# Remainders of prefetched weight units: subtraction on VectorE replaced by a negated copy on ScalarE and an accumulating transfer

## The chip, the core and the metric

The kernel runs on one core of a Trainium2 chip. The metric is the device time of the whole kernel in microseconds (us). Engines are named as in the profile: PE is TensorE, DVE is VectorE, ACT is ScalarE, POOL is GpSimd, SP is SyncE. In this kernel SP computes nothing: it issues transfers, in order.

## What is computed

A decoder trunk of two layers on 512 tokens of width 1024, in float32. Cut to what matters:

```
for l in range(2):
    h = x * (1 + scale1) + shift1
    u, q, k, v = split(h @ w_in[l])                 # 512 columns each
    ssm = s5_mixer(u)                               # state space scan, GELU, GLU with glu_w (512 x 512)
    att = diff_attention(rotary(q), rotary(k), v)   # 4 heads, two softmax maps each, causal
    mix = concat(ssm, att) @ w_out[l]
    x = layer_norm(alpha * x + (1 + gate1) * mix)
    h = x * (1 + scale2) + shift2
    x = layer_norm(alpha * x + (1 + gate2) * (silu(h @ w_gate) * (h @ w_up)) @ w_down)
```

The shifts, scales and gates are columns of `silu(c) @ mod_w[l] + mod_b[l]`.

## The kernel before, in words

Each matrix product is done as three matmuls in a rounded float32 format. Every operand X is split into a rounded part `hi` and a remainder `lo = X - hi`, and `mm3` (line 115) adds hi·hi, hi·lo and lo·hi in PSUM.

The weights come as 184 units of 128 x 1024 floats (512 KB), 92 for each layer. `wunit` (line 263) makes one: SP issues the load of `wraw` (two buffers), ACT rounds it into `whi` (five buffers; the helper `cp` on line 113), and DVE subtracts, `wlo = wraw - whi` (five buffers; the helper `tt`, line 104). A table `plo` gives the subtraction of four units of layer 1 to POOL. A buffer of `wraw` is free for the next load when the subtraction has read it.

`prefetch` calls `wunit` ahead of use, for 14 units of each layer: eight for the q and k columns (two for each head; the first has the weight rows of the lower four of eight k tiles, the second those of the upper four), two for the GLU, four for the output projection. `units(n)` hands the oldest ones out. All other units, those of u, v and of the feed-forward part, call `wunit` directly.

The mixer of a layer weaves three streams: the projections (PE), the S5 scan (`s5_gen`: small matmuls `kps`, `utp`, `qps`, `vps`, `yps` with chains of DVE and POOL work between them), and attention (`att_gen`). `tick()` is called between pieces of projection and starts whatever the table `PLAN` has due: a step of `s5`, of `att`, of the modulation columns (`mod`, each a 512 KB load `mraw` and a DVE reduction), or one `pf`, a prefetch. The framework then orders the instructions of each engine by its own schedule, so the order on an engine differs from that in which the code calls them.

SP's queue carries the unit loads `wraw` (line 265), the modulation loads `mraw` (294), small transfers of the S5 scan (`M<-kd` 544, `kd<-ksb` 475, `csl<-sC` 649) and others. A transfer that must wait for a buffer or for data holds all behind it on SP. POOL issues some transfers too (`sQ`, `sG`, `xs`, `gd`).

Of the kernel before, what the change touches and what calls it, by code (L numbers as in the profile page):

```python
# [14 lines left out]
ALU = mybir.AluOpType  # L15
# [7 lines left out]
OPT = {'MQ': 'sync', 'MODQ': 'sync', 'q_bld': 1, 'q_s5': 0, 'q_att': 0, 'q_pf': 0, 'CSQ': 'scalar', 'plo': [[1, 0, 1, 0, 0, 0, 0, 0, 0, 0, 0, 0, 0, 0, 0, 0, 0, 0], [0, 0, 0, 0, 0, 0, 1, 1, 1, 0, 0, 0, 0, 1, 0, 0, 0, 0]]}  # L23
# [39 lines left out]
def trunk_kernel(tc, xT, x, c, pos, modw, modb, wst, s5a, s5bc, s5d, glub, lamv, subw, lng, lnr, out):  # L63
    nc = tc.nc
    from contextlib import ExitStack

    with ExitStack() as es:
# [35 lines left out]
        def tt(out, a, b, op, eng=None):  # L103
            (eng or nc.vector).tensor_tensor(out, a, b, op=op)  # L104
# [7 lines left out]
        def cp(out, in_, scale=1.0):  # L112
            nc.scalar.activation(out, in_, AF.Copy, scale=scale)  # L113
# [9 lines left out]
        def f(ap):  # L123
            return ap.bitcast(F32)
# [135 lines left out]
                nc.gpsimd.dma_start(kd[l][:, :, 128:240].rearrange("q p x -> p q x"), zb)  # L260


        def wunit(idx, eng=None):
            raw = wp.tile([P, 1024], F32, tag="wraw", name="wraw", bufs=2)
            nc.sync.dma_start(raw, wst[idx])
            hi = wp.tile([P, 1024], F32R, tag="whi", name="whi", bufs=5)
            cp(hi, raw)
            lo = wp.tile([P, 1024], F32R, tag="wlo", name="wlo", bufs=5)
            tt(lo, raw, f(hi), ALU.subtract, eng=eng)
            return hi, lo  # L270

        ahead = []

        def prefetch(*idx):
            ahead.extend(wunit(i, nc.gpsimd if i % W0 < 22 and OPT["plo"][i // W0][i % W0 - 4] else None) for i in idx)

        def units(n):
            r = ahead[:n]
# [603 lines left out]
        W0 = 92  # L882
# [52 lines left out]
        for l in range(L):  # L935
# [7 lines left out]
            if l == 0:  # L943
# [35 lines left out]
                with queued(marks(), (POOL,)), strict():  # L979
                    first_x(0)  # L980
                    uw[0] = wunit(wb)
                    first_h(0)
                    first_l(0)
                    first_x(1)
                    for k in range(NK):
                        kp = k // 2
                        for t in range(NT):
                            mm3(ups[t], kt(hT, k, tok(t)), rows(uw[kp], k % 2), k == 0, k == 7)
                        if k + 1 < NK:
                            first_h(k + 1)  # L990
                        if k % 2 == 0 and k + 2 < NK:
                            uw[kp + 1] = wunit(wb + kp + 1)
                        if k + 2 < NK:
                            first_x(k + 2)
                        if k + 1 < NK:
                            first_l(k + 1)
                        for c_ in START[k]:
                            if c_ == "v":
                                vw.append(wunit(wb + 4 + len(vw)))
                            elif c_ == "V":  # L1000
                                first_v()
                            elif c_ == "c":
                                s5_rot(0, rots.pop(0), pms[0])
                            elif c_ == "p":
                                next(par, None)
                            elif c_ == "r":
                                next(rope, None)
                            elif c_ == "b":
                                next(bld)
                            else:  # L1010
                                mods_bg(cols, 2, "A2")
# [36 lines left out]
            def tick():  # L1048
                while plan and plan[0][0] < now[0] + 1:
                    kind = plan.pop(0)[1]  # L1050
                    if kind == "att":
                        with queued(marks()) if OPT["q_att"] else nullcontext():
                            next(attg, None)
                    elif kind == "s5":
                        with queued(marks(), (POOL,)) if OPT["q_s5"] else nullcontext():
                            next(s5g, None)
                    elif kind == "pf":
                        with queued(marks()) if OPT["q_pf"] else nullcontext():
                            prefetch(wb + pfs.pop(0))
                    elif kind == "cs":  # L1060
                        with queued(marks() if OPT["q_bld"] else m0, (POOL,)):
                            if rots:
                                s5_rot(0, rots.pop(0), pms[0])
                    elif kind == "bld":
                        with queued(marks() if OPT["q_bld"] else m0, (POOL,)):
                            next(bld, None)
                    else:
                        mods_bg(cols, 1, now[1])
                now[0] += 1
# [292 lines left out]
```

## Time and profile before

| what | value |
|---|---|
| median of 3 runs | 1278.39 us (1275.9 to 1282.51) |
| profiled execution, its time | 1279.54 us |
| its span | 1277.8 us |
| mean granted clock of PE over the span | 0.976 of full speed |
| PE busy | 1190.9 us, 93% of the span |
| DVE busy | 841.6 us, 66% |
| ACT busy | 478.9 us, 37% |
| POOL busy | 206.4 us, 16% |

The span is the time from the first to the last recorded instruction; 1.74 us of the profiled execution's time lie outside it. The busy shares are means over stages that have different limits. The mixer of layer 0 runs until about 260 us, its feed-forward part follows; the mixer of layer 1 lies between about 690 and 865 us.

### The profile page before, as it was taken

To read this page: it belongs to the slowest core of one execution; us is meant where nothing else is said; L and a number is where in the kernel's file an instruction comes from. 1 tells how busy PE (TensorE), PEld (TensorE's weight loads), DVE (VectorE), ACT (ScalarE), POOL (GpSimd) and SP (SyncE) were. 2 spreads that over 40 slices of the span, in tenths; PEclk is the share of its full clock that TensorE was granted. 3 is DMA by queue.
4 is the path that set the end of the run, shared out by engine and by line. 5 is a ranking of instruction groups with operands and counts; after the bars stand their busy time and mean duration, and the time that the engine had idled before them with its cause. 6 is when DMAs were issued, how large, how long until landed. Compare 5 with 4: busy or idle time off the path is not lost.

```text
span 1277.8 us, 17430 instructions
## 1 busy us (share of the span) xinstructions
PE 1190.9 (93%) x6608; PEld 992.1 (78%) x6608; DVE 841.6 (66%) x1537; ACT 478.9 (37%) x846; POOL 206.4 (16%) x286
## 2 busy tenths in 40 slices
PE   4768888999999999989899999999999999999997
PEld 3557777688888888867687798878888888888885
DVE  6679999866687576698647557785666222235556
ACT  3413446527322222243346245661733222234330
POOL 8943320001002121132001131100000000000001
PEclk8887999999999999999899999999999999999999
DMA  9654236534665666744333554423463333333241
GB/s 357 226 153 143 65 82 226 158 107 152 195 221 186 226 200 193 252 141 146 117 99 101 186 168 107 131 83 99 151 196 103 98 96 100 99 99 115 66 133 66
DMA packets 66868, 186.57 MB, mean 146 GB/s; under 512 B 7936, under 2 KB 21536, under 8 KB 66784
## 3 DMA queue, kind: packets, MB, share of 16 engines
q1 hardware_dynamic: 62352, 174.88, 43.4%
q0 software_dynamic: 2848, 8.70, 2.1%
q10 hardware_dynamic: 1584, 1.88, 0.5%
q8 instruction: 52, 0.85, 0.3%
q14 instruction: 32, 0.26, 0.1%
HBM read 171.85 MB, written 11.49 MB: 143 GB/s over the span
## 4 chain that ended last, share of the span: by engine, by line
PE 68%; DVE 18%; DMA 4%; POOL 3%; issue 3%; ACT 3%; SPq 0%; DVEq 0%; POOLq 0%; ACTq 0%
PE gps L116 37%; PE dps L116 14%; PE ops L116 4%; PE vps L116 3%; DVE mraw L110 3%; PE ups L116 2%; PE qkps L116 2%; DVE wlo L104 2%; DVE stmp L104 1%; POOL s5tmp L104 1%; DMA mraw<-in_modw 1%; DMA wraw<-in_wst 1%; DVE Gt L104 1%; PE yps L116 1%; PE glups L116 1%
## 5 line engine op out<-in xcount | busy, mean ns | idle before, releaser
L104 DVE TENSOR_TENSOR wlo<-wraw,whi 128x1024 fp32r<-128x1024 f32 x180 | 225.3, 1254 | 266.3 <-ACT whi L113 264.4
L113 ACT ACTIVATE whi<-wraw 128x1024 fp32r<-128x1024 f32 x184 | 194.2, 1058 | 376.6 <-PE gps L116 273.0
L116 PE MATMUL gps<-hT2h,whi 128*128 128x512 f32 (+1 forms) x768 | 286.4, 373 | 0.2
L116 PE MATMUL gps<-hT2l,whi 128*128 128x512 f32 (+1 forms) x768 | 285.7, 372 | 0.0
L116 PE MATMUL gps<-hT2h,wlo 128*128 128x512 f32 (+1 forms) x768 | 285.3, 372 | 0.0
L116 PE MATMUL dps<-whi,ah 128*128 128x512 f32 x704 | 223.7, 397 | 8.2 <-DVE rtmp L104 4.5
L116 PEld LDWEIGHTS gps<-hT2h,whi 128*128 128x128 f32 x768 | 144.6, 188 | 25.8 <-DVE rtmp L104 0.6
L116 PEld LDWEIGHTS dps<-whi,ah 128*128 128x128 f32 x704 | 133.9, 190 | 39.5 <-DVE rtmp L104 6.0
L116 PEld LDWEIGHTS gps<-hT2h,wlo 128*128 128x128 f32 x768 | 144.7, 188 | 25.1
L116 PEld LDWEIGHTS gps<-hT2l,whi 128*128 128x128 f32 x768 | 144.7, 188 | 24.9
L116 PE MATMUL dps<-wlo,ah 128*128 128x512 f32 x352 | 138.5, 393 | 0.0
L110 DVE SCALAR_TENSOR_TENSOR mraw<-mraw,scb 128x1024 f32<-128x1024 f32 x96 | 122.0, 1299 | 1.8 <-DMA mraw<-in_modw 1.6
L113 ACT ACTIVATE ah<-aT 128x512 fp32r<-128x512 f32 x88 | 53.8, 627 | 115.5 <-PE dps L116 93.2
L104 DVE TENSOR_TENSOR ah<-aT,ah 128x512 fp32r<-128x512 f32 x88 | 61.1, 706 | 40.0 <-ACT ah L113 39.6
L116 PEld LDWEIGHTS dps<-wlo,ah 128*128 128x128 f32 x352 | 67.2, 191 | 13.6
L116 PE MATMUL qkps<-whi,hTh 128*128 128x256 f32 x128 | 39.7, 312 | 7.3 <-ACT whi L113 6.5
L116 PE MATMUL ops<-whi,am 128*128 128x512 f32 x128 | 43.4, 398 | 0.0
L116 PE MATMUL qkps<-wlo,hTh 128*128 128x256 f32 x128 | 40.0, 313 | 0.5 <-DVE wlo L104 0.5
L104 POOL TENSOR_TENSOR rs<-rs,mhalf 128x1 f32<-128x1 f32 x16 | 10.8, 676 | 176.8 <-DVE rs L101 176.8
L116 PE MATMUL qkps<-whi,hTl 128*128 128x256 f32 x128 | 39.1, 306 | 0.0
L751 ACT ACTIVATE e<-sps,nm 128x128 f32<-128x128 f32 (+3 forms) x64 | 33.1, 525 | 14.9 <-DVE nm L749 12.8
L116 PE MATMUL qkps<-whi,hTnh 128*128 128x256 f32 x128 | 37.4, 292 | 0.0
(290 smaller groups left out, 1939.4 us busy)
## 6 DMA issues: line engine op xcount, KB each, us to landing
wraw<-in_wst SPq DMA_DIRECT2D x184, 512.0 KB, 3.7
mraw<-in_modw SPq DMA_DIRECT2D x96, 512.0 KB, 4.8
M<-kd SPq DMA_DIRECT2D x64, 64.0 KB, 3.6
gb<-in_lnr SPq DMA_DIRECT2D x8, 512.0 KB, 4.1
xT<-in_xT SPq DMA_DIRECT2D x8, 256.0 KB, 7.1
u<-us SPq DMA_DIRECT2D x32, 64.0 KB, 2.5
csl<-sC SPq DMA_DIRECT2D x8, 256.0 KB, 2.8
x<-in_x SPq DMA_DIRECT2D x4, 512.0 KB, 4.1
```

Of the source, the lines that this page charges most:

```text
L104: (eng or nc.vector).tensor_tensor(out, a, b, op=op)
L110: nc.vector.scalar_tensor_tensor(out, a, s, b, op0=ALU.mult, op1=ALU.mult, accum_out=acc_out)
L113: nc.scalar.activation(out, in_, AF.Copy, scale=scale)
L116: nc.tensor.matmul(ps, a, b, start=start, stop=stop)
L751: nc.scalar.activation(e[:, m, :n], ps[:, m, :n], AF.Exp, bias=nm[:, m : m + 1], accum_out=ss[:, i, m : m + 1])
```

## The change

The 28 prefetched units get their remainder another way. ACT writes `wlo = -whi` (a copy with scale -1 of the rounded part), and POOL issues a transfer that adds `wraw` onto it in place, from SBUF to SBUF. The value is the same. The other 156 units keep the subtraction on DVE; the branch for POOL's four goes with `prefetch`'s call.

```diff
-        def wunit(idx, eng=None):
+        def wunit(idx, eng=None, dma=False):
             raw = wp.tile([P, 1024], F32, tag="wraw", name="wraw", bufs=2)
             nc.sync.dma_start(raw, wst[idx])
             hi = wp.tile([P, 1024], F32R, tag="whi", name="whi", bufs=5)
             cp(hi, raw)
             lo = wp.tile([P, 1024], F32R, tag="wlo", name="wlo", bufs=5)
-            tt(lo, raw, f(hi), ALU.subtract, eng=eng)
+            if dma:
+
+                cp(lo, f(hi), scale=-1.0)
+                nc.gpsimd.dma_start(f(lo), raw, accum_op=ALU.add)
+            else:
+                tt(lo, raw, f(hi), ALU.subtract, eng=eng)
             return hi, lo
 
         ahead = []
 
         def prefetch(*idx):
-            ahead.extend(wunit(i, nc.gpsimd if i % W0 < 22 and OPT["plo"][i // W0][i % W0 - 4] else None) for i in idx)
+            ahead.extend(wunit(i, dma=True) for i in idx)
```

The lines of the kernel after are those of before plus 5 behind this place.

The scheduler moves instructions. SP, in the mixer of layer 0, where the loads for the last head (head 3) and for the GLU stand. Before, the `wraw` x2 of the second row are both units of head 3, and the last row is the GLU's two:

```order
L475 DMA kd_125<-ksb 128x128
L265 DMA wraw<-in_wst 128x1024 x2
L544 DMA M<-kd_125 16x8x128
L649 DMA csl<-sC 128x512
L544 DMA M<-kd_125 16x8x128 x5
L294 DMA mraw<-in_modw 128x1024
L544 DMA M<-kd_125 16x8x128 x2
L294 DMA mraw<-in_modw 128x1024
L265 DMA wraw<-in_wst 128x1024 x2
```

After, `wraw` x2 is the second unit of head 2 and the first of head 3; the next single `wraw` is head 3's second, and the last row is the first of the GLU's:

```order
L265 DMA wraw<-in_wst 128x1024 x2
L480 DMA kd_125<-ksb 128x128
L549 DMA M<-kd_125 16x8x128 x3
L654 DMA csl<-sC 128x512
L549 DMA M<-kd_125 16x8x128 x4
L299 DMA mraw<-in_modw 128x1024
L549 DMA M<-kd_125 16x8x128
L265 DMA wraw<-in_wst 128x1024
L299 DMA mraw<-in_modw 128x1024
L265 DMA wraw<-in_wst 128x1024
```

Head 3's second load has moved behind all eight `M` transfers, `csl` and one `mraw`.

On POOL, at the start of layer 1's mixer, the transfers for head 0's two units stand right behind the attention's `lve`, and those of the next units where the subtractions given to POOL stood.

PE, first matmuls of head 0 in layer 1, where the k tiles 4 and 5 (second unit) follow 2 and 3 (first unit). Before (`hTnh_4885` holds k tiles 2 and 3, `hTnh_4886` 4 and 5):

```order
L116 MATMUL qkps<-wlo,hTnh_4885 128x256
L116 MATMUL qkps<-whi,hTnl_4889 128x256
L116 MATMUL qkps<-whi,hTnh_4886 128x256
L116 MATMUL qkps<-wlo,hTnh_4886 128x256
L116 MATMUL qkps<-whi,hTnl_4890 128x256
```

After (`hTnh_4898` holds k tiles 0 and 1, `hTnh_4899` 2 and 3, `hTnh_4900` 4 and 5):

```order
L116 MATMUL qkps<-wlo,hTnh_4899 128x256
L116 MATMUL qkps<-whi,hTnl_4903 128x256
L116 MATMUL qkps<-whi,hTnh_4900 128x256
L116 MATMUL qkps<-wlo,hTnh_4898 128x256
L116 MATMUL qkps<-whi,hTnl_4902 128x256
```

Before, the second unit's `wlo` is read 12 matmuls after head 0's first; now PE first takes the 12 matmuls of the first unit for a second token tile, so it is read 24 after.

## Rows read from the trace of the kernel before

**Rows 1.** The page: span, and busy time of each engine.

```profile
span 1277.8 us, 17430 instructions
PE 1190.9 (93%) x6608; PEld 992.1 (78%) x6608; DVE 841.6 (66%) x1537; ACT 478.9 (37%) x846; POOL 206.4 (16%) x286
```

**Rows 2.** Busy by stretch (from:to us): PE, PEld, DVE, ACT, POOL, clock, DMA share, GB/s.

```profile
100.00:260.00 160.00, 139.56 (x1154) 118.21 (x1153) 147.96 (x320) 78.00 (x191) 34.05 (x32) 0.95 0.45 135
740.00:860.00 120.00, 114.30 (x976) 100.44 (x975) 88.23 (x204) 67.58 (x170) 21.11 (x25) 1.00 0.43 122
```

**Rows 3.** The same view, `wlo` alone: PE, PEld, DVE, POOL, clock, DMA share, GB/s.

```profile
100.00:260.00 160.00, 48.23 (x149) 29.62 (x149) 15.82 (x13) 0.00 (x0) 0.95 0.45 135
740.00:860.00 120.00, 44.03 (x146) 27.49 (x145) 10.91 (x9) 9.75 (x4) 1.00 0.43 122
```

**Rows 4.** Groups by form: count, busy us, mean ns, idle before and its releasers.

```profile
L104 DVE TENSOR_TENSOR wlo<-wraw,whi 128x1024 fp32r<-128x1024 f32 x180 | 225.3, 1254 | 266.3 <-ACT whi L113 264.4 <-DMA M<-kd 1.5
...
L113 ACT ACTIVATE whi<-wraw 128x1024 fp32r<-128x1024 f32 x184 | 194.2, 1058 | 376.6 <-PE gps L116 273.0 <-DMA wraw<-in_wst 77.5 <-PE dps L116 10.1
...
L104 POOL TENSOR_TENSOR wlo<-wraw,whi 128x1024 fp32r<-128x1024 f32 x4 | 9.8, 2438 | 21.6 <-ACT whi L113 21.6
```

**Rows 5.** The chain of waits, layer 0's mixer: start us, us, what.

```profile
96.73 1.24 DVE wlo L104
...
180.84 1.13 DVE wlo L104
...
198.82 1.14 DVE wlo L104
```

**Rows 6.** The chain of waits, layer 1's mixer.

```profile
738.00 11.53 PE qkps L116 x96
...
777.10 1.23 DVE wlo L104
...
824.41 1.13 DVE wlo L104
```

**Rows 7.** The timeline of ACT in three places: start us, us, operation, idle before.

```profile
95.64 1.06 ACT L113 ACTIVATE whi<-wraw 128x1024 fp32r<-128x1024 f32 x1 [1.34 <-issue]
...
188.33 0.60 ACT L113 ACTIVATE qkt<-qkps 128x512 f32<-128x512 f32 x1 [1.10 <-PE qkps L116]
...
736.57 1.05 ACT L113 ACTIVATE whi<-wraw 128x1024 fp32r<-128x1024 f32 x1
```

**Rows 8.** Transfers by issue: queue, count, KB each, median us to landing.

```profile
wraw<-in_wst SPq DMA_DIRECT2D x184, 512.0 KB, 3.7
...
sQ<-Q POOLq DMA_DIRECT2D x4, 512.0 KB, 5.6
...
gd<-mods POOLq DMA_DIRECT2D x4, 4.0 KB, 10.3
```

**Rows 9.** The timeline of PE, 96 to 140 us; in brackets the idle time ahead.

```profile
98.01 0.58 PE L116 MATMUL qkps<-wlo,hTh 128*128 128x256 f32 x1 [0.47 <-DVE wlo L104]
...
112.42 0.59 PE L470 MATMUL kps<-Gt,s5bc 128*32 128x112 f32 x16 [2.16 <-DVE stmp L104]
...
116.47 1.98 PE L615 MATMUL yps<-M,UU 128*64 128x128 f32 x16 [1.30 <-ACT ksb L113]
...
136.86 0.59 PE L470 MATMUL kps<-Gt,s5bc 128*32 128x112 f32 x16 [3.87 <-DVE Gt L104]
```

**Rows 10.** SP's timeline around head 3's loads.

```profile
183.73 0.35 SPq L294 DMA_DIRECT2D mraw<-in_modw  x1
184.13 0.91 SPq L544 DMA_DIRECT2D M<-kd  x2
```

**Rows 11.** The timeline of POOL at layer 1's start.

```profile
732.20 0.72 POOL L104 TENSOR_TENSOR lve<-ebase,lvs 128x2 f32<-128x2 f32 x1 [13.17 <-DVE lvs L709]
```

**Rows 12.** PE's waits, 55 to 300 us: total us, times, longest.

```profile
PE kps L470 <- DVE Gt L104: 10.8, 3, 4.2
```

**Rows 13.** SP's waits, 90 to 260 us.

```profile
SPq L265 <- DVE wlo L104: 18.4, 7, 4.1
```

## The prediction, before the changed kernel was run

> **What bounds the kernel now.** I read the page's busy line first. PE works 93% of the span, DVE 66%, ACT 37% [rows 1], so over the whole kernel PE sets the time, and a subtraction taken off DVE is worth something only where DVE ends last. The change touches the two mixers alone, so I cut the trace there [rows 2]. In 100 to 260 us (mixer of layer 0) DVE is busy 147.96 of 160 us and PE 139.56: here DVE bounds, and PE's 20.4 us of idle time are waits for it. In 740 to 860 us (mixer of layer 1) PE is busy 114.30 of 120 and DVE 88.23: here PE bounds, and DVE has room. The feed-forward parts keep their units and their order. The same stretches for `wlo` alone [rows 3] give what DVE would lose: 15.82 us in 13 subtractions in layer 0, 10.91 us in 9 in layer 1, where POOL loses 9.75 us in 4.
>
> **What is removed.** Of 180 subtractions on DVE at 1.25 us and 4 on POOL at 2.44 us [rows 4], 24 and 4 go. The ceiling for layer 0 is the 15.8 us of DVE work, if its stream were a single one that decides throughout. With the order kept, only a subtraction that the chain of waits goes through shortens it. In layer 0 there are three of them, 1.24 + 1.13 + 1.14 = 3.5 us [rows 5]; in layer 1 two, 1.23 + 1.13 = 2.4 us [rows 6]. The other 23 lie beside other work. That makes -5.9 us. The longer DVE gain I leave to a rival, since 13 x 1.22 us taken from a stream move its end only if DVE finds its next operands ready.
>
> **What is added on ACT.** 28 copies of 128x1024, priced as the rounding copy, 1.06 us each [rows 4]: 29.7 us, half of it in each mixer. ACT is busy 78.00 of 160 and 67.58 of 120 us [rows 2], so its idle time hides them except in the path of one unit, which becomes longer: rounding, negated copy, transfer, matmul, where it was rounding, subtraction, matmul.
>
> **What a transfer takes.** No row of before has an accumulating transfer or one from SBUF to SBUF. Nearest are transfers of the same 512 KB: unit loads from SP land after 3.7 us, `sQ` from POOL after 5.6 us [rows 8]. The slowest that POOL issues is `gd`, 10.3 us [rows 8]. I take 5.6 (same size, same queue) and keep 3.7 and 10.3 as bounds, as nothing excludes either. A remainder is then ready 1.06 + 5.6 = 6.7 us after its rounding in place of 1.25 us: 5.4 us later. POOL, busy 34.05 of 160 and 21.11 of 120 us [rows 2], has time to issue 14 transfers in each; what it loses, four subtractions, is more in layer 1 than what it gets. Where units are prefetched long ahead, the 5.4 us are hidden. Three places are not like that.
>
> *Layer 0, head 0, second unit.* Its rounding ends at 95.64 + 1.06 = 96.70 us [rows 7], PE wants the remainder at 98.01 - 0.47 = 97.54 and gets it at 98.0 [rows 9]. After: 96.70 + 1.06 + 5.6 = 103.4, that is 5.4 us later than now (3.5 to 10.1 by the bounds). Right behind, PE stands idle for DVE three times, 2.16 + 1.30 + 3.87 = 7.3 us by 137 us [rows 9]. DVE doesn't wait for head 0 there, but for its own scan work, so a late PE finds these operands ready. Price 0; if the cover is gone, 5.4; at the slow bound 10.1 - 7.3 = 2.8.
>
> *Layer 0, head 3, second unit.* SP now loads it behind an `mraw` and the `M` transfers. Those were issued at 183.73 and 184.13 us [rows 10], so the load goes out at about 184.6, lands 3.7 later (188.3), is rounded and negated by 190.4 and added by 196.0. Head 2's last copy on ACT starts at 188.33 [rows 7], PE then has 12 matmuls of the first unit at 0.12 us (11.53 us for 96, rows 6) and wants the remainder at 189.8: 6.2 us of waiting (4.3 to 10.9 by the bounds). But with DVE lighter, what SP waits for at the `M` transfers comes earlier, too. I take half, +3.1, with ends 0 and 10.9.
>
> *Layer 1, head 0.* POOL can't issue before `lve` ends, 732.20 + 0.72 = 732.9 [rows 11]; the first unit is there at 738.5, and PE begins at 738.0 [rows 6]. The second unit's rounding ends at 736.57 + 1.05 = 737.6 [rows 7], plus 1.06 and 5.6 is 744.3. PE's new order puts 24 matmuls ahead, 738.0 + 24 x 0.12 = 740.9. So it waits 3.4 us in all (1.5 to 8.1 by the bounds), and since PE bounds this stretch they are on the path: +3.4.
>
> **The sum.** -5.9 + 0 + 3.1 + 3.4 = +0.6 us on the profiled execution's 1279.54, that is 1280.1. That execution lies 1.15 us above the median of 1278.39, so as a median 1279.0. A difference of 0.5% (6.4 us: 1272.0 to 1284.8) is about what a measurement of this kernel can tell from no change. Forecast: no measurable change, 1279 us.
>
> **Rival 1, faster: DVE's relief is passed on.** If DVE's stream in layer 0 really decides, the scan's `Gt` comes earlier and PE's waits for it [rows 12] shrink: 10.8 us in three, of which the 4.2 before 100 us stay, as no subtraction is taken from DVE ahead of them, and 6.6 go. With head 3's load early (0 in place of 3.1): -5.9 - 6.6 + 0 + 3.4 = -9.1, as a median 1269.3 us. For it: DVE at 147.96 of 160. Against: PE, at 139.56, is 8 us behind it, so it becomes the bound soon, and a scan step also needs ACT, SP's transfers and PE.
>
> **Rival 2, slower: the transfer is slow and holds the raw buffers.** Only two `wraw` buffers exist, and each is now held until the transfer has landed. SP already waits 18.4 us in seven pieces for the subtraction to give one back, at most 4.1 [rows 13]; with 5.4 us more for each, `mraw`, `M` and `csl` stand behind it, so that head 3's half is not given back. For a landing time X the three places cost max(0, X - 7.5), X + 0.6 and X - 2.2, less 5.9. That passes +6.4 from X = 7.0 on. At X = 9, between `sQ` and `gd`, it is 1.5 + 9.6 + 6.8 - 5.9 = +12.0, as a median 1290.4 us; at 10.3 it is +15.9, 1294.3. For it: landing times on POOL's queue scatter from 5.6 to 10.3 us, and DMA already runs at a share of 0.45 in that stretch [rows 2]. Against: rows of the same size lie at 3.7 and 5.6.
>
> The Trainium skill speaks against the change here: its page "Collectives: The Full Stack", section "The bandwidth ceiling: the fold count and why AG ≠ RS ≠ AR", says that a reduction runs at about half the rate of a copy, not because the addition takes time, but because two sources are read through the same ring for one write. No row of before shows an accumulation. By that rule an upper estimate of X would be twice the 5.6 us of `sQ`, 11.2 us, and the sum by the three terms above +18.6 us, about 1297 as a median.
>
> **Rival 3: the change does little because the scheduler puts it elsewhere.** The orders of DVE and PE differ over all of layer 0, so the places could be covered and the gains be uncovered at random. That ends near the forecast and is part of it.
>
> **How the numbers follow.** The forecast 0.40, Rival 1 0.28, Rival 2 0.32. My bounds of X straddle 7.0, so slower is a little above faster. The range takes in Rival 1 with a few us more (-12 us) and Rival 2 up to X of about 9.8 (+14 us): 1266 to 1293. The forecast's own range is 1272 to 1285.
>
> **What would show it.** In the profile after, the landing time of the `wlo` transfers on POOL's queue decides first: about 5.6 us carries the sum, above 7.0 Rival 2. DVE busy time in 100 to 260 should fall from 148 by about 16. PE should wait for a `wlo` transfer at about 98, 190 and 741 us, 5, 3 and 3 us long. PE's waits for `Gt` should stay (forecast) or shrink by 6.6 us (Rival 1). SP's waits at its `wraw` loads (line 265) should grow from 18.4 us by some 5 us a unit under Rival 2. I am wrong in kind if DVE's busy share falls and PE's waits for DVE do not, or if the feed-forward parts move.

## The result: 3% slower

The changed kernel takes 1317.64 us (median of 4 runs, 1314.99 to 1318.71), the one before 1278.45: a ratio of 1.030 (95% interval 1.028 to 1.032), 39 us slower. The forecast was 1279 us, and its range ended at 1293.

The page after, for [rows 1]: PE has 10.3 us more busy time with the same number of instructions, DVE 26.6 us less, ACT 27.0 more.

```profile
span 1316.6 us, 17480 instructions
PE 1201.2 (91%) x6608; PEld 1001.7 (76%) x6608; DVE 815.0 (62%) x1513; ACT 505.9 (38%) x874; POOL 217.7 (17%) x310
```

The first thing to do with two such traces is to cut both at the same points of the program: the end of layer 0's u projection (PE at 60.5 us), the first feed-forward matmul of layer 0, a point 5.5 us after the first matmul of layer 1's mixer, and the last output projection of layer 1. Busy time by stretch of the kernel before (from:to us; PE, PEld, DVE, ACT, POOL, clock, DMA share, GB/s):

```profile
60.50:298.50 238.00, 205.00 (x1487) 171.92 (x1485) 204.86 (x437) 102.92 (x233) 57.42 (x62) 0.94 0.45 132
298.50:692.00 393.50, 382.80 (x1892) 316.91 (x1889) 280.01 (x480) 132.94 (x193) 60.12 (x67) 0.99 0.55 176
692.00:905.00 213.00, 204.42 (x1428) 173.61 (x1427) 145.04 (x323) 105.66 (x237) 28.95 (x42) 1.00 0.41 124
905.00:1277.80 372.80, 364.17 (x1698) 303.92 (x1696) 175.31 (x238) 113.33 (x154) 6.04 (x9) 1.00 0.35 110
```

and of the changed kernel:

```profile
60.60:326.30 265.70, 210.67 (x1487) 177.84 (x1485) 192.31 (x423) 117.27 (x248) 68.57 (x76) 0.88 0.57 146
326.30:720.00 393.70, 382.61 (x1891) 316.75 (x1889) 278.97 (x480) 132.94 (x193) 58.47 (x67) 0.99 0.55 176
720.00:943.90 223.90, 208.85 (x1428) 177.22 (x1427) 132.84 (x312) 119.45 (x251) 30.78 (x52) 0.98 0.56 150
943.90:1316.60 372.70, 364.18 (x1698) 303.90 (x1696) 175.22 (x238) 113.45 (x154) 6.07 (x9) 0.99 0.35 110
```

The feed-forward parts are the same to 0.2 us. Layer 0's mixer is 27.7 us longer: PE's idle time there went from 33.0 to 55.0 us, and its busy time grew by 5.7 us at a granted clock of 0.88 in place of 0.94. Layer 1's mixer is 10.9 us longer (idle 8.6 to 15.1, busy 4.4 more). So some 10 of the 39 us are PE's own matmuls at a lower clock. Summed by what ended them, PE's waits in layer 0's mixer were 21.4 us for DVE and 11.3 for ACT; now they are 26.5 for DVE, 14.3 for ACT and 13.9 for remainders.

The stretches of [rows 2] read as follows now. The work has moved, so they no longer hold the same part of the program; DVE, at 147.96 of 160 us before, is busy for 116.85:

```profile
100.00:260.00 160.00, 120.22 (x1015) 104.17 (x1014) 116.85 (x262) 73.62 (x159) 41.93 (x43) 0.85 0.63 151
740.00:860.00 120.00, 108.36 (x894) 95.60 (x892) 58.81 (x152) 60.20 (x124) 19.70 (x35) 0.97 0.68 178
```

PE's waits, 55 to 300 us (total, times, longest), for [rows 12]:

```profile
PE qkps L116 <- DMA wlo<-wraw: 13.9, 4, 7.0
PE kps L475 <- DVE Gt L104: 9.4, 2, 4.7
PE qps L494 <- DVE gl L107: 6.5, 1, 6.5
```

The transfer itself landed about as assumed, for [rows 8]:

```profile
wlo<-wraw POOLq DMA_DIRECT2D x28, 512.0 KB, 5.9
```

And where PE waits for a remainder, from its timeline. In layer 0 these are the four waits, one for each of the heads 0 to 3; in layer 1 the two of head 0 (two more, of 0.36 and 1.12 us, belong to later heads). The prediction had priced head 0 and head 3 of layer 0 and head 0 of layer 1:

```profile
107.39 0.58 PE L116 MATMUL qkps<-wlo,hTh 128*128 128x256 f32 x1 [7.03 <-DMA wlo<-wraw]
...
127.29 0.48 PE L116 MATMUL qkps<-wlo,hTh 128*128 128x256 f32 x1 [3.27 <-DMA wlo<-wraw]
...
162.63 0.58 PE L116 MATMUL qkps<-wlo,hTh 128*128 128x256 f32 x1 [2.85 <-DMA wlo<-wraw]
...
217.69 0.38 PE L116 MATMUL qkps<-wlo,hTh 128*128 128x256 f32 x1 [0.71 <-DMA wlo<-wraw]
...
767.51 0.38 PE L116 MATMUL qkps<-wlo,hTnh 128*128 128x256 f32 x1 [0.60 <-DMA wlo<-wraw]
...
774.97 0.58 PE L116 MATMUL qkps<-wlo,hTnh 128*128 128x256 f32 x1 [4.34 <-DMA wlo<-wraw]
```

These waits sum to 13.9 and 6.4 us in the two mixers, half of the 39. The rest isn't in them, so the trace alone doesn't settle the cause.

### The profile page after: what moved, and what is told of

The parts are those of the page before. It is cut to its first block, busy times and chain, and to the rows that moved or that the text cites. A ratio compares the mean times of both kernels' runs of the same rounds, so it can differ in the third digit from the quotient of the medians.

```text
span 1316.6 us, 17480 instructions
## 1 busy us (share of the span) xinstructions
PE 1201.2 (91%) x6608; PEld 1001.7 (76%) x6608; DVE 815.0 (62%) x1513; ACT 505.9 (38%) x874; POOL 217.7 (17%) x310
## 4 chain that ended last, share of the span: by engine, by line
PE 65%; DVE 15%; DMA 9%; ACT 4%; issue 4%; POOL 3%; SPq 0%; DVEq 0%; ACTq 0%; POOLq 0%
PE gps L116 36%; PE dps L116 14%; PE ops L116 4%; DMA wraw<-in_wst 4%; DVE mraw L110 2%; DMA wlo<-wraw 2%; PE qkps L116 2%; PE vps L116 2%; DVE wlo L104 2%; PE glups L116 1%; PE ups L116 1%; POOL s5tmp L104 1%; DMA mraw<-in_modw 1%; PE sps L752 1%; DVE stmp L104 1%
## 5 line engine op out<-in xcount | busy, mean ns | idle before, releaser
L104 DVE TENSOR_TENSOR wlo<-wraw,whi 128x1024 fp32r<-128x1024 f32 x156 | 196.0, 1258 | 266.9 <-ACT whi L113 266.5
L110 DVE SCALAR_TENSOR_TENSOR mraw<-mraw,scb 128x1024 f32<-128x1024 f32 x96 | 122.5, 1304 | 14.8 <-DMA mraw<-in_modw 14.8
L116 PEld LDWEIGHTS dps<-wlo,ah 128*128 128x128 f32 x352 | 67.0, 190 | 13.7
L116 PE MATMUL qkps<-wlo,hTh 128*128 128x256 f32 x128 | 40.9, 320 | 13.9 <-DMA wlo<-wraw 13.9
L272 POOL DMA_DIRECT2D wlo<-wraw x28 | 24.6, 880 | 136.4 <-ACT wlo L113 101.4
L116 PE MATMUL qkps<-wlo,hTnh 128*128 128x256 f32 x128 | 38.1, 298 | 6.4 <-DMA wlo<-wraw 6.4
```

Of the source, the lines that this page charges most:

```text
L110: nc.vector.scalar_tensor_tensor(out, a, s, b, op0=ALU.mult, op1=ALU.mult, accum_out=acc_out)
L116: nc.tensor.matmul(ps, a, b, start=start, stop=stop)
L272: nc.gpsimd.dma_start(f(lo), raw, accum_op=ALU.add)
```

## The experiments

The change does two things at once: it replaces an operation, and by that makes the scheduler lay out all engines anew. Most experiments take these apart by holding engines to a given order: an ordering edge from each instruction to the next on its engine, without a semaphore, put in after the kernel is recorded. The exchanged operations themselves (subtraction, negated copy, transfer) stay free in e1, e2, e6, e10, e13 to e15, e17 and e18:

```
for a, b in zip(at, at[1:]):            # at: the engine's order, as indices of recorded instructions
    tc.add_manual_dep(own[b], own[a].name, NOSYNC, reason="held")
```

All at a glance. Time is the median in us, the ratio is to runs of the kernel before on the same chip with its 95% interval; "mixer 0" and "mixer 1" are read from the profiled run: the start of the first feed-forward matmul against 298.5, and from there to layer 1's last output projection against 606.5.

| run | order held | remainder of prefetched units | time | ratio | mixer 0 | mixer 1 |
|---|---|---|---|---|---|---|
| changed kernel | its own | transfer, 28 units | 1317.6 | 1.030 (1.028 to 1.032) | +27.8 | +11.1 |
| e1 | changed | subtraction | 1297.8 | 1.015 (1.013 to 1.018) | +17.1 | +1.5 |
| e2 | before (PE, ACT, SP) | transfer | 1323.9 | 1.036 (1.034 to 1.038) | +24.9 | +19.1 |
| e3 | changed | transfer of 1/8 | 1291.7 | 1.012 (1.009 to 1.014) | +12.1 | +3.0 |
| e4 | changed | plain copy | 1302.1 | 1.020 (1.017 to 1.022) | +19.6 | +1.7 |
| e5 | changed | transfer from `whi` | 1323.4 | 1.037 (1.034 to 1.039) | +31.6 | +16.5 |
| e6 | before (PE, ACT, SP) | transfer of 1/8 | 1305.9 | 1.022 (1.021 to 1.024) | +16.4 | +9.2 |
| e7 | free | transfer, 12 late units | 1290.4 | 1.010 (1.008 to 1.012) | +9.1 | +0.8 |
| e8 | free | transfer, layer 1 alone | 1293.1 | 1.013 (1.011 to 1.015) | -0.9 | +14.8 |
| e9 | changed | transfer; `gd` in rows | 1313.5 | 1.026 (1.025 to 1.028) | +18.8 | +14.9 |
| e10 | changed | subtraction; `gd` in rows | 1297.1 | 1.013 (1.011 to 1.015) | +15.2 | +1.2 |
| e11 | before, `gd` later | as before | 1282.9 | 1.003 (1.001 to 1.005) | +2.5 | +1.0 |
| e12 | changed, `gd` later | transfer | 1311.6 | 1.025 (1.023 to 1.027) | +19.6 | +12.7 |
| e13 | PE as changed | subtraction | 1301.8 | 1.017 (1.013 to 1.021) | +20.3 | +3.0 |
| e14 | SP as changed | subtraction | 1284.4 | 1.004 (1.002 to 1.005) | +4.4 | +0.4 |
| e15 | that of e2 | subtraction | 1295.1 | 1.012 (1.010 to 1.014) | +13.7 | +1.8 |
| e16 | changed | none, copy alone | 1292.4 | 1.009 (1.006 to 1.013) | +6.0 | +0.9 |
| e17 | before (all) | transfer, 12 late units | 1296.1 | 1.013 (1.011 to 1.015) | +13.1 | -1.6 |
| e18 | before (all) | transfer, 6 late units of layer 0 | 1298.4 | 1.015 (1.013 to 1.016) | +17.2 | +1.0 |

The kernel before, held to its own order and otherwise unchanged, was not run. But e18, held on all engines, agrees with it where both do the same work: 937 matmuls in 108.4 and 108.2 us up to 195 us, and layer 1's mixer within 1.0 us. So the hold by itself shows no price there. The two mixer columns are from one run each: e17 and e18 have the same layer 0 in the same order and read +13.1 and +17.2, so some 4 us between two rows mean little.

### Order or transfer: e1 to e4

e1, the subtraction in the changed kernel's order; the hold stands on all engines:

```diff
-                cp(lo, f(hi), scale=-1.0)
-                nc.gpsimd.dma_start(f(lo), raw, accum_op=ALU.add)
+                tt(lo, raw, f(hi), ALU.subtract, eng=eng)
```

> The subtraction on VectorE and GpSimd is back for all 28 units, but every engine keeps the order that the changed kernel has (PE and SP row for row). Theory T (the remainder comes late and the raw buffers are held; the order by itself is cheap): 1276 to 1290 us, PE's waits for wlo gone, the raw loads of layer 0's heads 1 and 2 a few us earlier. Rival O (the new order by itself, with the raw loads of the heads behind M, csl and mraw, costs most of it): 1300 to 1318 us, with PE's long waits around 100 and 155 us still there.

It lies between the two ranges: half of the 39 us is there with no transfer in the kernel. T, by which the order is cheap, fails, and so does O, by which it costs most of the 39. In layer 0's mixer PE is idle for 10.4 us more than before, and its matmuls take 6.6 us more at a mean granted clock of 0.90 in place of 0.94.

e2, the changed kernel with PE, ACT and SP held to the order of before:

> The new remainders, but PE, ScalarE and SP keep the order of the kernel before (VectorE and GpSimd are left to the scheduler). Theory T: 1300 to 1318 us, as slow as the change, since each remainder still comes some 5 us later and the raw buffer is held as long. Rival O: 1278 to 1290 us.

Slower than the changed kernel and above both ranges, so Rival O fails as the whole cause. With e15 below, the exchange of the subtraction for the transfer costs 29 us in this order and 20 in the changed one (1317.6 against e1's 1297.8): the new order makes some room for the late remainders. So the prices of order and transfer depend on each other.

e3 and e4 keep the changed kernel's order on every engine and change only the transfer:

```diff
-                nc.gpsimd.dma_start(f(lo), raw, accum_op=ALU.add)
+                nc.gpsimd.dma_start(f(lo)[:, 0:128], raw[:, 0:128], accum_op=ALU.add)   # e3
+                nc.gpsimd.dma_start(f(lo), raw)                                          # e4
```

> Every order as in the changed kernel, but the transfer adds only the first 128 of 1024 columns (the remainders of the other seven eighths lack the raw part). Theory T, if the landing time is mostly bytes: landing near 3 us in place of 5.9 and 1290 to 1305 us; if the landing time is mostly fixed: landing near 5 and 1308 to 1318 us. Rival O: 1312 to 1318 us whatever the landing time. A third, B (14 MB of extra traffic slows the other transfers): wraw and mraw land earlier, and time falls by more than PE's waits for wlo.

> Every order as in the changed kernel, but the transfer copies the raw unit over the negated part instead of adding it (the remainders are the raw units). If the addition is what makes the transfer slow (two reads for one write), landing falls from 5.9 to about 4 us and time to 1300 to 1310 us; if not, landing stays at 5.5 to 6 and time at 1313 to 1319 us.

Landing of e3's transfer:

```profile
wlo<-wraw POOLq DMA_DIRECT2D x28, 64.0 KB, 3.3
```

of e4's:

```profile
wlo<-wraw POOLq DMA_DIRECT2D x28, 512.0 KB, 4.7
```

e3 lies in Theory T's range for a landing that goes by the bytes, and e4 in its first range: the price follows the bytes, and the addition. Rival O's 1312 to 1318 us fails. Theory B is not borne out by the loads: in e3 `wraw` and `mraw` land after 3.7 and 4.9 us (medians), as in the changed kernel. But the time falls by 25.9 us and PE's waits for remainders by 12.6 alone (20.3 to 7.7).

An addition lands only 1.2 us later than a copy of the same bytes, yet costs 15.5 us more. With the copy, PE's waits for remainders are 13.3 us in place of 20.3, and SP's waits for the transfers, 80 to 330 us, 22.6 in place of 37.8. What differs more than the landing is how long it occupies the DMA engines. The page's line on POOL's queue has packets, MB and the share of 16 engines' span; before:

```profile
q0 software_dynamic: 2848, 8.70, 2.1%
```

after:

```profile
q0 software_dynamic: 6880, 23.38, 8.2%
```

and with the plain copy, e4:

```profile
q0 software_dynamic: 6880, 23.38, 5.3%
```

8.2% of 1316.6 us less 2.1% of 1277.8 is 81 us for 28 transfers, 2.9 us of all 16 engines each; for the copy (5.3% of 1300.3) it is 42 us, 1.5 each. The same bytes take 1.9 times as long when they are added. The Trainium skill states such a factor in "Collectives: The Full Stack", section "The bandwidth ceiling: the fold count and why AG ≠ RS ≠ AR", for a reduce-scatter against an all-gather, which copies: half the rate, as two sources are read for one write. This case agrees with the factor (1.9); that two sources are read, no run here shows. On landing it would have misled, since 4.7 became 5.9 and not twice as much. Which part of the 15.5 us comes from this occupancy, and which from later remainders and longer held buffers, was not separated. POOL pays too: an issue takes it 880 ns for the addition, 557 for the copy.

### What DVE's relief is worth: e16

e16 keeps the changed order and the negated copy, and drops the transfer.

> Every order as in the changed kernel, with the negated copy but without any transfer (the remainders lack the raw part). Against the first experiment (1297.8 us) this is what taking 24 subtractions off VectorE and 4 off GpSimd is worth with nothing in their place but the copy. If VectorE bounds layer 0's mixer: 1280 to 1288 us. If its relief is not passed on: 1292 to 1299 us.

Against e1 it gains 5.4 us (its four runs scatter from 1286.6 to 1295.1, and the profiled one, whose mixers the table has, is the fastest, so this is 5.4 within a few us). PE's waits for DVE in layer 0's mixer are 22.5 us in place of e1's 28.8. e3, with a short transfer, is level with it. The relief is small, and not far above the scatter.

### Raw buffer or lateness: e5 and e6

e5 adds `whi` in place of `wraw`, so ACT's rounding alone frees the raw buffer:

```diff
-                nc.gpsimd.dma_start(f(lo), raw, accum_op=ALU.add)
+                nc.gpsimd.dma_start(f(lo), f(hi), accum_op=ALU.add)
```

> Every order as in the changed kernel and a transfer of the same size and kind, but it adds the rounded part instead of the raw unit (the remainders come out as zero), so a raw buffer is free once ScalarE has rounded it. Theory H (what costs is that the transfer holds the two raw buffers and with them SP's queue): 1298 to 1306 us, SP's waits for wlo (37.8 us in 80 to 330) gone. Theory L (what costs is that PE gets the remainder late): 1312 to 1319 us, PE's waits for wlo unchanged.

Neither: SP's waits for the transfers are gone, and the kernel is 5.8 us slower still. Transfers and raw loads now both land later, in layer 0's mixer after 7.5 and 5.2 us (medians) in place of 6.5 and 4.2. Over both layers:

```profile
wlo<-whi POOLq DMA_DIRECT2D x28, 512.0 KB, 7.2
```

PE's waits for a remainder in layer 0's mixer grew from 13.9 to 20.1 us. So here letting the raw buffers go early gained nothing. That the held buffer had kept loads and transfers apart is a reading of the landing times, and not shown by a run of its own.

e6 puts e3's short transfer into e2:

> PE, ScalarE and SP in the order of the kernel before, and the transfer adds only the first 128 of 1024 columns (the rest of the remainders lacks the raw part). In the changed kernel's order the short transfer was 6 us faster than the subtraction; if that is VectorE's relief and holds here too: 1268 to 1276 us. If the order of before has no room for even a 3.3 us landing: 1282 to 1300 us.

Far off the first, beyond the second: 1305.9 us. The short transfer doesn't pay in this order either, though PE waits only 6.1 us for its remainders in both mixers. DVE's and POOL's orders are the scheduler's own in e2 and e6, which e15 weighs for e2: its order with the subtraction.

> The subtraction, every engine in the order that the second experiment had (PE, ScalarE and SP as before, VectorE and GpSimd as the scheduler put them there). If the second experiment's 46 us are the transfer's: 1276 to 1284 us. If they lie in VectorE's and GpSimd's order: 1300 us or more.

1295.1 us, between the two again. So of e2's 46 us some 17 are DVE's and POOL's order, and 29 the transfer's. For e6 this split was not run, so how much of its 29 us is DVE's and POOL's order stays open. The order of before on all five engines with all 28 transfers was not run either.

### Which units, which layer: e7 and e8

```diff
-            ahead.extend(wunit(i, dma=True) for i in idx)
+            ahead.extend(wunit(i, <as before>, dma=i % W0 >= 16) for i in idx)   # e7
+            ahead.extend(wunit(i, <as before>, dma=i >= W0) for i in idx)        # e8
```

> Only the six units per layer for the GLU and the output projection take the transfer, the eight of the heads keep the subtraction; the scheduler orders everything anew. Theory L (lateness at PE): these units are prefetched further ahead, 1274 to 1284 us. Theory H (held raw buffers): 1285 to 1300 us, as their loads follow each other on SP between the modulation loads.

> Only layer 1 takes the transfer, layer 0 keeps the subtraction; the scheduler orders everything anew. If the stages are independent as the two traces read (layer 0's mixer 27.7 us longer, layer 1's 10.9): 1286 to 1292 us. If a shift of order in layer 0 makes part of it by chance: outside that, 1278 to 1284 or over 1296 us.

e8 came out 1 us above its range: layer 0 is left as it was (-0.9), layer 1 costs +14.8. e7 is inside Theory H's range: 13 us for units that PE never waits for. Its order is new as well, which e17 takes out.

### A neighbour: e9 to e12

The chain of waits of the changed kernel has a raw load of 15 us in it, and behind that the head's next remainder:

```profile
91.58 6.86 DMA wraw<-in_wst
...
100.90 6.44 DMA wlo<-wraw
...
139.15 14.95 DMA wraw<-in_wst
...
156.90 5.68 DMA wlo<-wraw
```

Just ahead of that load POOL issues layer 0's gate vector, 4 KB in 1024 pieces of 4 bytes:

```profile
137.89 0.98 POOL L315 DMA_DIRECT2D gd<-mods  x1 [1.67 <-DVE ksb L107]
```

In the kernel before it went out at 128.2 us, and SP issued nothing from 124.6 to 139.3. e9 (changed kernel) and e10 (e1) write the four gate vectors as 128 rows of 32 bytes:

```diff
-            nc.gpsimd.dma_start(gd.rearrange("k p -> p k"), mods[:, l, 24 * w + 16 : 24 * w + 24])
+            nc.gpsimd.dma_start(gd.rearrange("k p -> (k p)").rearrange("(p k) -> p k", p=P), mods[...])
```

> Every order as in the changed kernel, but the four gate transfers gd write 128 rows of 32 bytes in place of 1024 pieces of 4 bytes (the gate's columns come out permuted). Theory C (in the new order layer 0's gd goes out at 137.9 us, just beside the raw load of 139.2, which then lands after 15 us in place of 4): that load lands after 4 to 5 us, 1304 to 1309 us. If the load's 15 us are no more than a wait that something else would replace: 1313 to 1318 us.

> The first experiment (the changed kernel's order with the subtraction) with the same gate transfers in 128 rows of 32 bytes (the gate's columns permuted). Theory C: its raw load at 137.0 us took 13.5 us as well, so 1285 to 1290 us, which leaves the order itself some 10 us. If the order is dear for other reasons: 1294 to 1298 us.

In e9 that load lands after 4.5 us, and 4.2 us of 39 come back (the intervals of the two ratios just overlap); in e10 nothing does, although the load of e1 had taken 13.5 us as well. e11 and e12 move layer 0's `gd` alone, in the kernel before into the way of `kd`, `M` and `mraw`, in the changed kernel out of it:

> The kernel before, every order held, but GpSimd issues layer 0's gd some 6 us later, behind four operations of the scan, so that it flies while SP issues kd, M and mraw at 139 to 141 us. Theory C: kd lands after 6 to 10 us in place of 1.6, and the kernel takes 1283 to 1290 us. If the 4-byte pieces do no harm to what is issued behind them: 1276 to 1280 us.

> The changed kernel, every order held, but GpSimd issues layer 0's gd behind the next accumulating transfer and one operation of the scan, at about 150 to 160 us. Theory C: the raw load of 139 lands in 4 to 5 us and the gain stays unless gd meets the M transfers there: 1305 to 1312 us. Otherwise 1314 to 1320 us.

In e12 it goes out here, and the kernel gains 6.0 us; e11 loses 4.1. The raw load that e12 issues 0.9 us behind it, at 155.5, lands after 12.1 us, so the delay has moved to another load:

```profile
154.63 1.00 POOL L315 DMA_DIRECT2D gd<-mods  x1
```

Theory C holds in kind and not in size. e12 is inside its range and e11 at its lower edge, but e9 and e10 lie in the other one: a load of 15 us on the chain was worth 4 to 6 us and not the 10 by which it was late, as if other waits took its place.

### PE's order or SP's: e13 and e14

> The subtraction everywhere, and only PE held in the changed kernel's order; the other engines are left to the scheduler. If PE's order (scan steps earlier, attention later) is what made the first experiment 20 us slower: 1292 to 1300 us. If it was SP's order (the heads' raw loads behind M, csl and mraw): 1277 to 1285 us.

> The subtraction everywhere, and only SP held in the changed kernel's order; the other engines are left to the scheduler. If SP's order made the first experiment slower: 1292 to 1300 us; if PE's: 1277 to 1285 us. Both above 1290 would say that either forces the other.

PE's order, with the other engines scheduled anew around it, gives all of e1's loss (1301.8 us, just above its range), SP's about 6 us; PE's decides. What may be dear in it can be read from e1: PE's operations of the attention after 240 us. Before (count, busy us, mean ns):

```profile
L747 PE MATMUL sps<-qk 64*128 64x128 f32 (+2 forms) x20 | 3.4, 360 | 0.0
L116 PE MATMUL po<-v,wT 128*128 128x128 f32 x20 | 3.0, 281 | 0.0
```

e1:

```profile
L752 PE MATMUL sps<-qk 64*128 64x128 f32 (+2 forms) x30 | 5.1, 412 | 0.0
L116 PE MATMUL po<-v,wT 128*128 128x128 f32 x34 | 5.1, 286 | 0.0
```

The new order took scan steps forward among head 0's and 1's projections and left attention for the end, where little else is left to fill PE's waits. From the start of the output projection to the feed-forward part e1 needs 73.2 us, before 58.4. That this tail is the whole of the 20 us was not tried.

### The late units with the old order: e17 and e18

> The transfers only for the six GLU and output projection units of each layer, and every engine in the order of the kernel before. In e7 the same twelve transfers with a new order took 1290.4 us. If e7's 12 us were its order: 1274 to 1280 us, and with VectorE relieved of twelve subtractions a gain of up to 3 us is possible. If the late remainders and held raw buffers of these units cost by themselves: 1285 to 1292 us.

> As the run before, but only for the six units of layer 0, where VectorE is busiest; every engine in the order of the kernel before. If the transfers there are hidden: 1273 to 1279 us, the best version the runs point to. If not: 1281 to 1288 us.

Both lie beyond even their slow ranges, and no version run here beats the kernel before. e18 is the cleanest sight of the transfer's own price: all five engines run in the order of before, the first 195 us agree, six transfers follow, PE waits for none of them, and the kernel takes 19 us longer. Of the 17.2 us in layer 0's mixer 8.8 are idle time of PE and 8.4 its own matmuls: from 195 us on, the same 552 take 105.0 us at a mean granted clock of 0.90, where they took 96.8 at full speed (1.00), with PE idle for 15.7 us in place of 6.7. Its chain of waits, start and duration:

```profile
190.26 4.51 DMA wraw<-in_wst
...
197.38 7.69 DMA wlo<-wraw
205.07 0.02 SPq L265
...
205.14 4.68 DMA wraw<-in_wst
...
218.97 0.30 SPq L265
...
219.37 5.97 DMA mraw<-in_modw
...
227.98 6.55 DMA mraw<-in_modw
```

SP wants the third raw buffer, has to wait for the first transfer to land (205.07), and issues the load at 205.1 where it was 200.0 before; the fifth and sixth loads of this run go out at 218.9 and 227.6 in place of 209.3 and 215.4. The modulation loads `mraw` stand behind them in SP's queue, and DVE, whose order is held, stands before its reduction of them. DVE's waits for `mraw`, 180 us to the mixer's end, before:

```profile
DVE mraw L110 <- DMA mraw<-in_modw: 1.6, 2, 0.9
```

e18:

```profile
DVE mraw L110 <- DMA mraw<-in_modw: 14.8, 5, 4.9
```

So the raw buffers do cost here what e5 didn't show for the changed kernel's order. Both are seen here: in which of two ways a late transfer is paid seems to depend on what stands behind it.

## Why the prediction was wrong

**What held.** The landing was near (5.6 taken, 5.9 measured; 6.5 in layer 0's mixer), and so was layer 1's head 0 (3.4 predicted, 0.60 + 4.34 measured). ACT's copies, all present in e16, did not eat up the relief. The relief's size agrees (5.9 predicted, 5.4 in e16 against e1), but in part by luck: the 5.9 were five subtractions on the old order's chain of waits, 2.4 of them in layer 1, and there e16 and e1 differ by 0.6 us.

**What didn't.** Head 0 of layer 0 was priced at 0, and at 5.4 without its cover; it waited 7.0 us. The cover is there, as the waits of PE at 112, 116 and 137 us [rows 9] are gone from the list, but one of 6.5 us for DVE came in at 158. (Of the three covering waits, the one of 1.30 us was for ACT and not for DVE, as the row says; and of PE's 20.4 us of idle time in 100 to 260 us 16.5 were waits for DVE and 3.7 for ACT.) The prediction's own sign of being wrong in kind came true: DVE's busy share of layer 0's mixer fell from 86% to 72%, and PE's waits for DVE rose from 21.4 to 26.5 us. So DVE's load by itself did not set the length of that mixer: with 16.7 us less of it in an unchanged order (e16 against e1) about 5 came back.

**First failing step: the order at nothing.** Rival 3 put the reordering of PE and DVE down as places that are "covered" or "uncovered at random", near the forecast. By e1 it costs 20 us, and e13 shows that PE's order, with the other engines scheduled around it, is enough for that. The prediction read three places in the new order and took the rest for noise around zero. But every other order that was run with the subtraction was slower: e1, e10, e13, e14 and e15 lie 6 to 23 us above. A likely reason, not shown, is `PLAN`: it gives its places to seven decimals, as if fitted to the kernel before, and the change left it as it was. A plan fitted to the transfers was not run, so the runs don't tell how fast the changed kernel can become.

**Second failing step: "Where units are prefetched long ahead, the 5.4 us are hidden."** By this only three places had a price, and the formula of Rival 2 gave 0 + 6.5 + 3.7 - 5.9 = +4.3 us at the measured 5.9; it set the point from which the transfer hurts at 7.0. The three places were priced at 6.5 us in all; PE waited 20.3 us for remainders, 6.1 of them at heads 1 and 2 of layer 0, which had no price, and 0.7 at head 3, which had 3.1. In the changed kernel's order the transfer costs 25 us (1317.6 against e16's 1292.4). Rival 2 named the way, two buffers and SP's queue behind them, but priced only the remainders, not the other passengers of that queue. e18 shows these, `mraw` first, for units whose remainders PE never waits for.

**What wasn't seen.** That adding costs 15.5 of the 25 us (e4), with the DMA engines occupied 1.9 times as long as by the copy; `gd` in the way of a load (4 to 6 us of the sum, e9 and e12); and the clock: the prediction counts waits alone, but of the 38.6 us in the two mixers 10.1 are the same number of matmuls at a lower mean clock (0.88 for 0.94, and 0.98 for 1.00).

The ledger, each step a difference of two medians (before, e1, e16, e4, after): 1278.45, +19.3 for the order, -5.4 for DVE's relief, +9.8 for a plain transfer of the bytes, +15.5 for adding instead of copying: 1317.64. It adds up by construction, and it is one path: by way of e15 and e2, the order that DVE and POOL have there costs 17 us, the exchange 29, and the change of all orders from there to the changed kernel's gives 6 back.

## What to carry to other kernels

Where a scheduler lays out the engines, price the new order as a term of its own: hold the old order, or give the old operation the new one, before a time is put down to the operation. A transfer in place of an engine's operation is paid at places that its landing time doesn't show: the buffer that it reads stays taken, and the queue that wants that buffer stops with all that is behind it (e18). An accumulating transfer also takes 2.9 us of all 16 DMA engines here, against 1.5 for a copy; what others lose by that was not separated. And the idle time that it causes can come with a lower clock for the matmuls around it. Taking 26.6 us of work off DVE gained about 5.

## What the runs showed of the hardware

- An accumulating transfer of 512 KB within SBUF, issued by POOL: landing 4.5 to 8.9 us, median 5.9; 2.9 us of all 16 DMA engines; 880 ns of POOL. A plain copy: 4.7 us, 1.5 us, 557 ns. An accumulating transfer of 64 KB lands after 3.3 us.
- 4 KB in 4-byte pieces delayed a 512 KB load issued 1.3 us later to 14.95 us; in rows of 32 bytes the load took 4.5 (e9). Issued later, they delayed the next load, 0.9 us behind them, to 12.1 (e12).
- Freeing the raw buffers earlier did not make the kernel faster: with the raw loads let go, the transfers landed after 7.2 us instead of 5.9, and the kernel took 5.8 us more (e5).
- Six transfers that PE waits for nowhere cost 19 us (e18): SP waited 32.0 us for them in 80 to 330 us, and PE's matmuls behind them ran at a mean granted clock of 0.90 where it had been 1.00.
